# A two-layer mixture-of-experts network: six pairs' outputs added in DRAM, and the experts' weights read in 16 KB runs

## The chip, the cores and the metric

The kernel runs on one core of one Trainium2 chip. The metric is device time in microseconds for one whole execution. The median of three runs before is 1957.69 us (1956.69 to 1958.7).

## The reference, cut to what matters

Two streams pass through two layers: 512 latent tokens `x` ("l") and 256 context tokens ("c"), 1024 wide, all in fp32. A layer is a token mixer (short convolution, retention, windowed attention) and then a mixture of 16 experts, in which each expert picks its own tokens. The second layer has no context stream after the mixer. The part that the change touches:

```
def expert_choice_ffn(h, w_router, w_gate, w_up, w_down):
    n_tok, d_model = h.shape[1], h.shape[2]
    cap = CAPACITY_FACTOR * n_tok // N_EXPERTS          # 64 latent or 32 context tokens per expert
    aff = jax.nn.softmax((h @ w_router).astype(jnp.float32), axis=-1)
    gate, idx = lax.top_k(jnp.swapaxes(aff, 1, 2), cap)
    xs = jax.vmap(lambda hb, ib: hb[ib])(h, idx)
    a = jnp.einsum('becd,edf->becf', xs, w_gate)
    u = jnp.einsum('becd,edf->becf', xs, w_up)
    y = jnp.einsum('becf,efd->becd', jax.nn.silu(a) * u, w_down) * gate[..., None].astype(h.dtype)
    def scatter(ib, yb):
        return jnp.zeros((n_tok, d_model), yb.dtype).at[ib.reshape(-1)].add(yb.reshape(-1, d_model))
    return jax.vmap(scatter)(idx, y)
...
        h_l = modulate(rms_norm(x, norm2_g[l]), sh2, sc2)
        x = x + g2 * expert_choice_ffn(h_l, w_router[l], w_gate[l], w_up[l], w_down[l])
        if need_ctx:
            h_c = modulate(rms_norm(ctx, norm2_g[l]), csh2, csc2)
            ctx = ctx + cg2 * expert_choice_ffn(h_c, w_router[l], w_gate[l], w_up[l], w_down[l])
```

Each expert has three weight matrices of 1024 x 1024 fp32, 4 MiB each: 201 MB a layer.

## The kernel before, in words

**Experts.** `experts` works on eight pairs of experts. A pair's 128 rows (64 tokens for each of its two experts) are one tile; in layer 0, 128 context rows serve two pairs. For a pair it runs three products: `gate`, `up` and `down`, each over eight slices of 128 of the contracted dimension (`matrix`, with `lat_mm` and, for the context, `cx_mm`). The tokens are the weights that TensorE holds, the experts' weights stream past them. `times` multiplies the activated gate by `up`, `turned` transposes the product (eight transposes, four more for the context), and `down` takes it from there. `columns` transposes gathered rows and `modulate` scales them into `xT`. TensorE's order in this stage is written out by hand (`manual_schedule`):

```
            for p in range(7):
                rows(p + 2)          # gathers, on POOL
                gate(p + 1)
                turned(p)
                silu(p + 1)
                if p:
                    add(p - 1)
                inputs(p + 2)
                down(p)
                up(p + 1)
            add(6)
            turned(7)
            if two:                  # layer 0
                down(7)
                add(7)
```

**Outputs.** `down` scales its result by the token's gate and `g2` and splits it into a high and a low part (`yH`, `yL`, `ycH`, `ycL`). `add` builds a one-hot matrix of the pair's token numbers on VectorE and multiplies it with both parts on TensorE: 16 matmuls for the latent tokens (L1295, L1296), 8 for the context (L1305, L1306), each pair of them added into the residual `xe` in SBUF by VectorE (L1297, L1308). In layer 0, `xe` is loaded from the residual's DRAM copy `xres_d` (L1317) ahead of the first pair.

**Inputs.** In layer 0 the normalised rows lie in DRAM (`xn_d`), and `gather` fetches a pair's rows by an indirect DMA from POOL (L1047); its two buffers are shared by latent and context rows. In layer 1 the scaled rows (`scaled`) stay in SBUF as `xn`, and `gather_pe` picks them by a one-hot product on TensorE (L1092).

**Weights.** A `Ring` of tiles of 2 MiB ([128, 4, 1024]) holds the experts' weights, six tiles in layer 0. `ring_loads` gives the order: `gate`, `up` of a pair, then the next pair's `gate`, then `down`; four tiles to a matrix. SP issues a load (L1422) when its tile has been read. Row 128 j + p of a half matrix goes to partition p, slot j (`"(j p) n -> p j n"`), in runs of 4 KB. Some late tiles of layer 1 are loaded slot by slot (L1428).

**Selection and start.** `Norm2` transposes the residual and multiplies by the router's weights, `top` finds each expert's tokens, `slots_l` and `slots_c` turn the lists into columns (`idx_l`, `idx_c` for the gathers, `slot_l`, `sidx_c`, `gate_c` for the outputs). The modulation vectors come from `mod_half` and `mod_gen` (`w_mod` in tiles of 512 KB); `mod_cols` transposes them into the columns `A2`, `B2` by which `modulate` scales. At the very start SP loads the tokens (L282) and then small rows (`c`, `c_ctx`, `norm1_g`, `norm2_g`, `conv_w`, `final_g`, L1469 to L1474), which one transpose (L1476) turns into `cols`; everything behind needs it.

Except in the experts' loop, a scheduler orders each engine's instructions by the program's order and the tiles' dependencies, and two DMAs that write the same DRAM tile wait for each other.

Of the kernel before, what the change touches and what calls it, by code (L numbers as in the profile page):

```python
# [59 lines left out]
GLATE = 1  # L60
FINE = (9, 10, 11, 12)
# [26 lines left out]
def kernel(ctx_stack: ExitStack, tc: tile.TileContext, x, c, ctx, c_ctx, w_mod, b_mod, norm1_g,  # L88
# [58 lines left out]
    mod_d = [[dram.tile([2, 2048], F32, name=f"mod{l}{b}") for b in range(3)] for l in range(2)]  # L147
    A1, B1, A2, B2 = ([[cst.tile([128, KC], F32, name=f"{n}{l}{s}") for s in "lc"] for l in range(2)]
# [89 lines left out]
    def mod_cols(l, b, m, pp):  # L238
        ps = pp.tile([128, 4, 4, 32], F32, name="ps_mc", tag="t", bufs=4)
        for s in range(4):  # L240
            PE.transpose(ps[:, s].rearrange("p q r -> p (q r)"), m[:, 128 * s:128 * s + 128], ident)
        for r in range(2):
            v = ps[:, :, :, r].rearrange("p s q -> p q s")

            def o(t):
                return t[l][r].rearrange("p (q s) -> p q s", q=2)

            def g(t):
                return t[l].rearrange("p (q s) -> p q s", q=2)
            if b == 0:  # L250
                DVE.tensor_copy(o(B1), v[:, 0:2])
                DVE.scalar_tensor_tensor(o(A1), v[:, 2:4], 1.0, g(n1col), op0=OP.add, op1=OP.mult)
            elif b == 1:
                DVE.tensor_copy(o(B2), v[:, 2:4])
            else:
                DVE.scalar_tensor_tensor(o(A2), v[:, 0:2], 1.0, g(n2col), op0=OP.add, op1=OP.mult)
# [633 lines left out]
    class Norm2:  # L890
# [9 lines left out]
        def half(self, nh):  # L900
            s, p, pp, x, R = self.s, self.p, self.pp, self.x, self.R
            for t in range(NT[s]):
# [4 lines left out]
                for j in range(4):  # L907
                    PE.transpose(ps[:, j], xs[:, 128 * j:128 * j + 128], ident)
# [33 lines left out]
        def scaled(self, xn):  # L942
            for t in range(NT[self.s]):
                ACT.activation(xn[:, t], self.x[:, t], AF.Copy, scale=self.m[:, 1, t:t + 1])
# [46 lines left out]
    def slots_l(rp, p, pp, R, lst):  # L991
# [17 lines left out]
        for a, src in enumerate((R.tok_l, va)):  # L1009
            for half in range(2):  # L1010
                PE.matmul(ps[64 * half:64 * half + 64, 8 * a:8 * a + 8], src, ident[0:16, half:16:2],
                          start=True, stop=True)
        R.idx_l = rp.tile([128, 8], I32, name="idx_l")
# [4 lines left out]
    def slots_c(rp, pp, R, lst):  # L1018
        val, fi = lst
        ps = pp.tile([128, 512], F32, name="ps_r", tag="r", bufs=1)  # L1020
        for q in range(4):
# [4 lines left out]
                      tile_position=(0, 32 * q))  # L1026
        R.idx_c = rp.tile([128, 4], I32, name="idx_c")
# [32 lines left out]
    def columns(l, s, xs, ep, nb, bank):  # L1060

        xT = ep.tile([128, KC, 128], F32, name="xT" + s, bufs=nb)
        for g in range(2):
            ps = bank("ps_t").rearrange("p (j n) -> p j n", j=4)
            for j in range(4):
                PE.transpose(ps[:, j], xs[:, (4 * g + j) * 128:(4 * g + j + 1) * 128], ident)
# [91 lines left out]
    def experts(l, ep, ring, pp, R, xe, streams, late):  # L1158
# [66 lines left out]
        def turned(p):  # L1225

            aT[p] = E[0].tile([128, KC, 128], F32, name="aT", tag="aT", bufs=1)
            for h in range(2):
                ps = ptile("ps_t", "x").rearrange("p (j n) -> p j n", j=4)
                for j in range(4):  # L1230
                    PE.transpose(ps[:, j], sil[p][:, 512 * h + 128 * j:512 * h + 128 * j + 128], ident)  # L1231
# [4 lines left out]
            if two:  # L1236
                ps = ptile("ps_t", "bc").rearrange("p (j n) -> p j n", j=4)
                for j in range(4):
                    PE.transpose(ps[:, j], silc[p][:, 128 * j:128 * j + 128], ident)
# [24 lines left out]

        def down(p, fill=None):
            Dn = [ptile("ps_d", "a") for _ in range(2)]
            DC = ptile("ps_dc", "ac") if two else None
            for _ in matrix(Dn, DC, aT[p], lambda k, e: aTc[p][:, k % 4, 2 * e + k // 4, :], fill=fill):
                pass
            yH = E[0].tile([128, D], F32R, name="yH", bufs=1)  # L1270
# [39 lines left out]
        with tc.manual_schedule(engines={mybir.EngineType.PE}):  # L1310
            if two:
# [4 lines left out]
                for s in streams:  # L1316
                    POOL.dma_start(xe[s], xres_d[s].rearrange("(t p) d -> p t d", p=128))  # L1317
# [20 lines left out]
            for p in range(7):  # L1338
# [4 lines left out]
                if p:  # L1343
# [30 lines left out]
    def ring_loads(l):  # L1374
# [3 lines left out]
        for wsrc, p in order:  # L1378
            for kh in range(2):
                for e in range(2):  # L1380
                    yield wsrc[l, 2 * p + e, 512 * kh:512 * kh + 512, :].rearrange("(j p) n -> p j n", p=128)
# [59 lines left out]
    for l in range(2):  # L1441
# [3 lines left out]
        if True:  # L1445
# [3 lines left out]
            POOL.dma_start(R.wr, w_router[l].rearrange("(j p) n -> p j n", p=128))  # L1449
# [13 lines left out]
            with ExitStack() as s2:  # L1463
                pp = s2.enter_context(tc.tile_pool(name=f"pp{l}", bufs=1, space=PSUM))
                m0 = router_cols(l, streams, pp, R) if l else None
                if l == 0:
# [5 lines left out]
                    SP.dma_start(rows[32:48], norm2_g.rearrange("l (r p) -> (l r) p", p=128))  # L1472
# [128 lines left out]
            with ExitStack() as s2:  # L1601
# [32 lines left out]
                def passes():  # L1634
# [23 lines left out]
                    def select_l():  # L1658
# [4 lines left out]
                        slots_l(rp, p, pp, R, lst)  # L1663
# [6 lines left out]
                    if two:  # L1670
# [16 lines left out]
                        def select_c():  # L1687
# [4 lines left out]
                            slots_c(rp, pp, R, (yield from top(p, pp, R, "c", 32)))  # L1692
# [109 lines left out]
```

## Time and profile before

| | us |
|---|---|
| median of 3 runs | 1957.69 |
| the profiled execution | 1955.63 |
| its span | 1953.8 |
| TensorE busy | 1815.8 (93%) |
| VectorE busy | 722.0 (37%) |
| ScalarE busy | 489.6 (25%) |
| GpSimd busy | 286.5 (15%) |

Times are in microseconds from the span's start unless ns is said. PE is TensorE's matmuls, PEld its weight loads, DVE VectorE, ACT ScalarE, POOL GpSimd, and SPq, POOLq the queues from which SP and GpSimd issue. A name such as `ps_d<-ring,aT` is output, then the streamed and the held operand. L1297 is line 1297 of the kernel. Matmuls overlap, so the sum of their durations is more than the time that they take; the starts of groups are the better measure.

### The profile page before, as it was taken

What the parts mean: (1) busy time and instruction counts of PE and PEld (TensorE: products, weight loads), DVE (VectorE), ACT (ScalarE), POOL (GpSimd) and SP (SyncE); (2) the same over time, 40 slices, a digit from 0 to 9 for tenths busy, and PEclk for the clock granted to TensorE, in tenths of its full rate; (3) what the DMA queues carried; (4) which work ended last, traced back from release to release, by engine and by line L of the source; (5) the groups of instructions that cost most, each with busy time, mean ns of one, the idle gap of its engine ahead of it and who ended that gap; (6) DMA issues with size and microseconds to landing.
All of it is one profiled execution on the core that took longest, in us unless ns stands there. A gap on an engine that the chain in (4) does not pass through costs nothing. (4 is left out here: it accounts for less than half of the span.)

```text
span 1953.8 us, 30558 instructions
## 1 busy us (share of the span) xinstructions
PE 1815.8 (93%) x12747; PEld 1040.3 (53%) x12747; DVE 722.0 (37%) x1785; ACT 489.6 (25%) x983; POOL 286.5 (15%) x309
## 2 busy tenths in 40 slices
PE   5899999999889999999999789999969999989986
PEld 2778777766423333333333488877744444433532
DVE  5645345663511213222223555446341122221214
ACT  3444343344201001001100345454321000000001
POOL 3323132343200000000000132323410000000000
PEclk9999999999889999999999999999979999999998
DMA  8453454267689999998897411211747999999994
GB/s 267 162 196 130 140 177 150 87 243 280 241 341 409 390 397 358 354 394 342 347 400 282 152 45 33 63 36 33 290 182 286 415 416 417 417 416 415 417 417 173
DMA packets 157761, 522.94 MB, mean 268 GB/s; under 512 B 8836, under 2 KB 31432, under 8 KB 157624
## 3 DMA queue, kind: packets, MB, share of 16 engines
q1 hardware_dynamic: 154200, 511.24, 68.4%
q0 software_dynamic: 3424, 9.75, 1.4%
q8 instruction: 100, 1.64, 0.3%
q14 instruction: 37, 0.30, 0.0%
HBM read 510.41 MB, written 10.55 MB: 267 GB/s over the span
## 5 line engine op out<-in xcount | busy, mean ns | idle before, releaser
L1102 PE MATMUL ps_g<-ring,xTl 128*32 128x512 f32 (+1 forms) x1472 | 244.3, 596 | 11.8 <-DMA ring<-in_w_gate_dram 10.5
L1102 PE MATMUL ps_u<-ring,xTl 128*32 128x512 f32 (+1 forms) x1536 | 236.7, 598 | 14.3 <-DMA ring<-in_w_up_dram 13.6
L1102 PE MATMUL ps_d<-ring,aT 128*32 128x512 f32 (+1 forms) x1536 | 234.7, 593 | 0.5 <-DMA ring<-in_w_down_dram 0.3
L1102 PEld LDWEIGHTS ps_g<-ring,xTl 128*32 128x32 f32 (+1 forms) x1472 | 75.7, 121 | 159.5 <-issue 133.1
L1102 PEld LDWEIGHTS ps_u<-ring,xTl 128*32 128x32 f32 (+1 forms) x1536 | 70.2, 120 | 168.0 <-issue 144.1
L351 PE MATMUL acc<-wH,hHl 128*128 128x256 f32 x512 | 151.6, 296 | 2.6 <-ACT wH L272 1.3
L352 PE MATMUL acc<-wH,hLl 128*128 128x256 f32 x512 | 144.7, 283 | 3.7 <-DVE hLl L341 3.7
L353 PE MATMUL acc<-wL,hHl 128*128 128x256 f32 x512 | 145.3, 284 | 1.2 <-DVE wL L273 1.1
L1102 PEld LDWEIGHTS ps_d<-ring,aT 128*32 128x32 f32 (+1 forms) x1536 | 68.6, 119 | 144.8 <-issue 142.4
L1235 ACT ACTIVATE aT<-ps_t 128x512 f32<-128x512 f32 x16 | 9.6, 598 | 495.3 <-PE ps_t L1231 495.3
L351 PEld LDWEIGHTS acc<-wH,hHl 128*128 128x128 f32 x512 | 97.4, 190 | 30.1 <-issue 23.7
L1274 DVE SCALAR_TENSOR_TENSOR ps_d<-ps_d,slot_l,g 128x512 f32<-128x512 f32 x32 | 24.3, 759 | 227.8 <-PE ps_d L1102 226.1
L1214 DVE TENSOR_TENSOR sil<-ps_u,sil 128x512 f32<-128x512 f32 x32 | 22.1, 692 | 232.6 <-PE ps_u L1102 232.6
L1233 DVE COPY aT<-ps_t 128x512 f32<-128x512 f32 x16 | 11.1, 691 | 261.8 <-PE ps_t L1231 261.8
L352 PEld LDWEIGHTS acc<-wH,hLl 128*128 128x128 f32 x512 | 97.5, 191 | 4.6 <-DVE hLl L341 4.6
L353 PEld LDWEIGHTS acc<-wL,hHl 128*128 128x128 f32 x512 | 97.5, 191 | 4.0 <-DVE wL L273 2.3
L273 POOL TENSOR_TENSOR wL<-wraw,wH 128x512 fp32r<-128x512 f32 x44 | 57.6, 1308 | 273.1 <-ACT wH L272 263.3
L675 DVE TENSOR_REDUCE mc<-ps_s 128x1 f32<-128x513 f32 (+2 forms) x80 | 55.2, 690 | 84.5 <-PE ps_s L672 52.7
L1275 ACT ACTIVATE yH<-ps_d 128x512 fp32r<-128x512 f32 x32 | 19.1, 597 | 263.9 <-DVE ps_d L1274 263.9
L677 ACT ACTIVATE P<-ps_s,mc 128x513 f32<-128x513 f32 (+2 forms) x80 | 55.1, 689 | 97.0 <-DVE mc L675 96.9
L1153 POOL TENSOR_TENSOR x<-z,xTl 128x512 f32<-128x512 f32 x3 | 4.2, 1413 | 512.4 <-ACT z L1152 512.4
L272 ACT ACTIVATE wH<-wraw 128x512 fp32r<-128x512 f32 x88 | 55.1, 629 | 90.2 <-PE acc L352 37.4
(482 smaller groups left out, 3393.7 us busy)
## 6 DMA issues: line engine op xcount, KB each, us to landing
ring<-in_w_up_dram SPq DMA_DIRECT2D x64, 2048.0 KB, 13.7
ring<-in_w_gate_dram SPq DMA_DIRECT2D x61, 2048.0 KB, 13.8
ring<-in_w_down_dram SPq DMA_DIRECT2D x61, 2048.0 KB, 16.0
wm<-in_w_mod_dram SPq DMA_DIRECT2D x96, 512.0 KB, 4.6
wraw<-in_w_in_dram SPq DMA_DIRECT2D x44, 512.0 KB, 3.7
wraw_o<-in_w_out_dram SPq DMA_DIRECT2D x24, 512.0 KB, 4.5
ring<-in_w_gate_dram SPq DMA_DIRECT2D x12, 512.0 KB, 5.6
ring<-in_w_down_dram SPq DMA_DIRECT2D x12, 512.0 KB, 14.7
```

What stands on the lines that cost most here:

```text
L272: ACT.activation(H, src, AF.Copy)
L273: sub_eng().tensor_sub(L, src, f32(H))
L351: PE.matmul(ps, aH, bH, start=start, stop=False)
L352: PE.matmul(ps, aL, bH, start=False, stop=False)
L353: PE.matmul(ps, aH, bL, start=False, stop=stop)
L675: DVE.tensor_reduce(mc[:, 0:1], sc, AX.X, OP.max, negate=True)
L677: ACT.activation(P[:, :nk + 1], sc, AF.Exp, bias=mc[:, 0:1], accum_out=mc[:, 1:2])
L1102: PE.matmul(G[h][c:c + n], lhs[:, k, c:c + n], W[e][:, j, 512 * h:512 * h + 512], start=(k == 0), stop=(k == KC - 1), tile_position=(0, c))
L1214: DVE.tensor_mul(sil[p][:, hs], U[h], sil[p][:, hs])
L1233: DVE.tensor_copy(aT[p][:, 4 * h:4 * h + 4], ps)
L1274: DVE.scalar_tensor_tensor(Dn[h], Dn[h], R.slot_l[:, 1, p:p + 1], R.g2[:, hs], op0=OP.mult, op1=OP.mult)
L1275: ACT.activation(yH[:, hs], Dn[h], AF.Copy)
```

## The change

The experts' outputs of pairs 0 to 5 in layer 0 are no longer added by TensorE: `down` ends in `scatter`, in which VectorE writes the scaled output as fp32 into SBUF and POOL issues four indirect DMAs (two experts, latent and context) that add the rows to the residual in DRAM. `xe` is loaded after pair 5's; pairs 6 and 7 are added as before. `slots_l` and `slots_c` make the index columns for it.

The experts' weights are laid out so that partition p holds rows 4 p to 4 p + 3 of a half matrix. What is contracted with them takes the same order: the transposes read every fourth element, the second norm's vector is loaded in that order, the router's weights too, and layer 1's `scaled` writes its rows in it.

```diff
+NACC = 6
...
     def mod_cols(l, b, m, pp):
-            PE.transpose(ps[:, s].rearrange("p q r -> p (q r)"), m[:, 128 * s:128 * s + 128], ident)
+            PE.transpose(ps[:, s].rearrange("p q r -> p (q r)"), m[:, s::4] if b else m[:, 128 * s:128 * s + 128], ident)
...
     class Norm2: half
-                    PE.transpose(ps[:, j], xs[:, 128 * j:128 * j + 128], ident)
+                    PE.transpose(ps[:, j], xs[:, j::4], ident)
         def scaled(self, xn):
             for t in range(NT[self.s]):
-                ACT.activation(xn[:, t], self.x[:, t], AF.Copy, scale=self.m[:, 1, t:t + 1])
+                o, i = xn[:, t], self.x[:, t]
+                if xn is not self.x:
+                    o, i = o.rearrange("q (g j p) -> q g j p", g=2, j=4), i.rearrange("q (g p j) -> q g j p", g=2, j=4)
+                ACT.activation(o, i, AF.Copy, scale=self.m[:, 1, t:t + 1])
...
     slots_l
+        if two:
+            PE.matmul(ps[0:64, 16:24], R.tok_l, ident[0:16, 1:16:2], start=True, stop=True)
+            R.to_l = two.tile([64, 2, 8], I32, name="to_l")
+            for e in range(2):
+                DVE.tensor_copy(R.to_l[:, e], ps[0:64, 16 * e:16 * e + 8])
         R.idx_l = rp.tile([128, 8], I32, name="idx_l")
...
     slots_c
+        R.to_c = ra.tile([64, 2, 8], I32, name="to_c")
+        for h in range(2):
+            hs = slice(32 * h, 32 * h + 32)
+            for e in range(2):
+                PE.matmul(ps[hs, 20 + 8 * e:28 + 8 * e], fi, ident[0:16, e:16:2], start=True, stop=True,
+                          tile_position=(0, 32 * h))
+        for e in range(2):
+            DVE.tensor_scalar(R.to_c[:, e], ps[0:64, 20 + 8 * e:28 + 8 * e], 2.0, hm[0:64, 0, 1:2], op0=OP.mult,
+                              op1=OP.subtract)
...
     columns
-                PE.transpose(ps[:, j], xs[:, (4 * g + j) * 128:(4 * g + j + 1) * 128], ident)
+                PE.transpose(ps[:, j], xs[:, 512 * g + j:512 * g + 512:4], ident)
     turned
-                    PE.transpose(ps[:, j], sil[p][:, 512 * h + 128 * j:512 * h + 128 * j + 128], ident)
+                    PE.transpose(ps[:, j], sil[p][:, 512 * h + j:512 * h + 512:4], ident)
-                    PE.transpose(ps[:, j], silc[p][:, 128 * j:128 * j + 128], ident)
+                    PE.transpose(ps[:, j], silc[p][:, j::4], ident)
...
+        def scatter(p, Dn, DC):
+            y = ep.tile([128, D], F32, name="y", tag=("yH", "yL")[p % 2], bufs=1)
+            yc = ep.tile([128, 512], F32, name="yc", tag=("ycH", "ycL")[p % 2], bufs=1)
+            for h in range(2):
+                hs = slice(512 * h, 512 * h + 512)
+                DVE.scalar_tensor_tensor(y[:, hs], Dn[h], R.slot_l[:, 1, p:p + 1], R.g2[:, hs], op0=OP.mult, op1=OP.mult)
+            DVE.scalar_tensor_tensor(yc, DC, R.gate_c[:, p:p + 1], R.g2c, op0=OP.mult, op1=OP.mult)
+            for e in range(2):
+                es = slice(64 * e, 64 * e + 64)
+                for dst, idx, src in ((xres_d["l"][:, :], R.to_l, y),
+                                      (xres_d["c"].rearrange("t (h n) -> (t h) n", h=2), R.to_c, yc)):
+                    POOL.indirect_dma_start(out=dst, out_offset=bass.IndirectOffsetOnAxis(ap=idx[:, e, p:p + 1], axis=0),
+                                            in_=src[es, :], in_offset=None, compute_op=OP.add)
+            if p == NACC - 1:
+                for s in streams:
+                    POOL.dma_start(xe[s], xres_d[s].rearrange("(t p) d -> p t d", p=128))
         down
+            if two and p < NACC:
+                scatter(p, Dn, DC)
+                return
...
     experts, ahead of pair 0 in layer 0
-                for s in streams:
-                    POOL.dma_start(xe[s], xres_d[s].rearrange("(t p) d -> p t d", p=128))
     experts, the loop
-                if p:
+                if p > (NACC if two else 0):
                     add(p - 1)
     ring_loads
-                    yield wsrc[l, 2 * p + e, 512 * kh:512 * kh + 512, :].rearrange("(j p) n -> p j n", p=128)
+                    yield wsrc[l, 2 * p + e, 512 * kh:512 * kh + 512, :].rearrange("(p j) n -> p j n", j=4)
...
-            POOL.dma_start(R.wr, w_router[l].rearrange("(j p) n -> p j n", p=128))
+            for kh in range(2):
+                POOL.dma_start(R.wr[:, 4 * kh:4 * kh + 4], w_router[l, 512 * kh:512 * kh + 512].rearrange("(p j) n -> p j n", j=4))
...
-                    SP.dma_start(rows[32:48], norm2_g.rearrange("l (r p) -> (l r) p", p=128))
+                    for i in range(4):
+                        SP.dma_start(rows[32 + 4 * i:36 + 4 * i], norm2_g[i // 2, 512 * (i % 2):512 * (i % 2) + 512]
+                                     .rearrange("(p j) -> j p", j=4))
```

## Rows read from the trace of the kernel before

**Rows 1.** The page's 40 slices: TensorE and the DMA engines, busy tenths.

```profile
PE   5899999999889999999999789999969999989986
...
DMA  8453454267689999998897411211747999999994
```

**Rows 2.** Windows: busy PE, PEld, DVE, ACT, POOL; PEclk, DMA share, GB/s.

```profile
1500.00:1900.00 400.00, 377.01 (x1884) 171.56 (x1880) 81.22 (x151) 30.39 (x59) 0.00 (x0) 0.98 1.02 416
575.00:1060.00 485.00, 484.78 (x4304) 173.75 (x4306) 108.55 (x197) 46.80 (x95) 7.51 (x8) 1.00 0.96 374
```

**Rows 3.** Timeline of TensorE in layer 0: start, length, instruction.

```profile
599.84 1.92 PE L1102 MATMUL ps_d<-ring,aT 128*32 128x512 f32 x16
...
620.47 1.90 PE L1102 MATMUL ps_u<-ring,xTl 128*32 128x512 f32 x16
...
663.18 0.50 PE L1295 MATMUL ps_s<-yH,OH 128*128 128x512 f32 x1
...
668.88 1.25 PE L1066 MATMUL ps_t<-ident,xsl 128*128 128x128 f32 x8
670.07 1.92 PE L1102 MATMUL ps_d<-ring,aT 128*32 128x512 f32 x16
...
741.34 1.92 PE L1102 MATMUL ps_d<-ring,aT 128*32 128x512 f32 x16
```

**Rows 4.** Timeline of TensorE in layer 1, first transposes of two pairs.

```profile
1624.94 1.09 PE L1231 MATMUL ps_t<-ident,sil 128*128 128x128 f32 x8
...
1685.37 1.09 PE L1231 MATMUL ps_t<-ident,sil 128*128 128x128 f32 x8
```

**Rows 5.** Waits in layer 1, 1490 to 1920: total, times, longest.

```profile
PEld ps_g L1102 <- DMA ring<-in_w_gate_dram: 16.0, 7, 3.5
...
PEld ps_u L1102 <- DMA ring<-in_w_up_dram: 7.6, 2, 4.0
```

**Rows 6.** Timeline around `turned` and its copies, layer 0.

```profile
598.39 0.66 PE L1066 MATMUL ps_t<-ident,xsl 128*128 128x128 f32 x4 [0.22 <-ACT aTc L1241]
...
1015.01 1.09 PE L1231 MATMUL ps_t<-ident,sil 128*128 128x128 f32 x8
...
1016.73 0.60 ACT L1241 ACTIVATE aTc<-ps_t 128x512 f32<-128x512 f32 x1
```

**Rows 7.** Line L1047, the gathers: duration min/median/max, and landing.

```profile
L1047 POOL DMA_INDIRECT xsl<-xn_l,idx_l x8: 935/942/1037, 503.5 to 882.0; - x8
...
DMA to landing us min/median/max: 4.2/7.9/8.8
```

**Rows 8.** Tile `ps_t`: weight loads of `turned`, ns min/median/max.

```profile
L1231 PEld LDWEIGHTS ps_t<-ident,sil x128: 138/140/144, 596.2 to 1912.7; 128*128 128x128 f32 x128
```

**Rows 9.** Tile `qsum` and line L935: VectorE's reductions of 64 elements.

```profile
L120 DVE TENSOR_REDUCE qsum<-ident x1: 240/240/240, 2.9 to 2.9; 128x16 f32<-128x64 f32 x1
...
L935 DVE TENSOR_REDUCE rm<-aff_l x2: 219/220/220, 482.5 to 1435.8; 128x4 f32<-128x64 f32 x2
```

**Rows 10.** DMA queues, 1500 to 1900: packets, MB, share of 16 engines.

```profile
DMA packets 41799, 166.22 MB, mean 416 GB/s; under 512 B 1267, under 2 KB 1267, under 8 KB 41780
...
q1 hardware_dynamic: 41780, 165.95, 102.2%
```

**Rows 11.** DMA queues from 1180 to 1230.

```profile
DMA packets 2115, 2.15 MB, mean 43 GB/s; under 512 B 64, under 2 KB 2112, under 8 KB 2112
...
q1 hardware_dynamic: 2112, 2.10, 13.3%
```

**Rows 12.** The page's packets over the whole span.

```profile
DMA packets 157761, 522.94 MB, mean 268 GB/s; under 512 B 8836, under 2 KB 31432, under 8 KB 157624
```

**Rows 13.** Waits of SP at the start, and the first transpose.

```profile
SPq L1474 <- DMA xt<-in_x_dram: 1.9, 1, 1.9
...
14.24 0.34 PE L1476 MATMUL ps_t<-ident,rows 68*128 68x68 f32 x1 [14.24 <-DMA rows<-in_final_g_dram]
```

**Rows 14.** Line L1014, the copy that makes `idx_l`.

```profile
L1014 DVE CAST idx_l<-ps_r x2: 153/160/167, 503.0 to 1452.2; 128x8 int32<-128x8 f32 x2
```

More of the change, by code (lines that the diff above doesn't have):

```diff
@@ L989, in top, with slots_l @@
         return val, fi
-    def slots_l(rp, p, pp, R, lst):
+    def slots_l(rp, p, pp, R, lst, two):
         val, fi = lst
@@ L1016, in slots_l, with slots_c @@
         DVE.tensor_copy(R.slot_l, ps[:, :16].rearrange("p (a e) -> p a e", a=2))
-    def slots_c(rp, pp, R, lst):
+    def slots_c(rp, pp, R, lst, ra):
         val, fi = lst
@@ L1662, in select_l @@
                         lst = yield from top(p, pp, R, "l", 64)
-                        slots_l(rp, p, pp, R, lst)
+                        slots_l(rp, p, pp, R, lst, two and ra[0])
                         if two:
@@ L1691, in select_c @@
                             yield from keep("c", nc2, xc)
-                            slots_c(rp, pp, R, (yield from top(p, pp, R, "c", 32)))
+                            slots_c(rp, pp, R, (yield from top(p, pp, R, "c", 32)), ra[0])
                         aft = select_c()
```

## The prediction

> **What bounds the kernel now.** I read the page's slices first [rows 1]: TensorE is busy nearly everywhere, while the DMA engines are full only in two stretches, slices 13 to 21 and 32 to 39. These are the expert stages of layer 0 and layer 1, so I then read the windows by stage [rows 2]. In layer 0's window TensorE is busy 484.78 of 485 us at 374 GB/s: TensorE bounds it. In layer 1's window the rate is 416 GB/s and the DMA share is over 1, while TensorE is idle for 23 of 400 us: the transfers bound it. Next came the timeline of TensorE. In layer 0 one pair takes 70.2 us where two gathered inputs are turned less, and 71.3 us where the context's rows are turned too (from 599.84, the start of a `down`, to 670.07 and 741.34 [rows 3]); the mean is 70.75. In layer 1 a pair takes 60.4 us (1624.94 to 1685.37 [rows 4]), and the waits view lists 23.6 us before weight loads that a ring transfer ended [rows 5]. The chain of waits agrees in kind: in layer 1 it runs back through ring transfers, in the last stage of selection through VectorE, so that whatever layer 0 gains or the start loses reaches the end in full, as layer 1's work begins with layer 0's residual.
>
> **Part 1: adds 0 to 5 leave TensorE.** `add` runs eight times in layer 0 and six go. One stands between the first L1295 and the next transpose: 663.18 to 668.88, 5.70 us [rows 3]. Nothing else runs on TensorE in that time, and TensorE is the bound, so 6 x 5.70 = 34.2 us go. VectorE's 12 adds, ACT's copies and the one-hot rows go too and are worth nothing, as both engines are idle most of that window (VectorE is busy 108.55 of 485 us [rows 2]).
>
> What is late next: the add also covered the copies of `turned` before `down`. ACT ends the copy of `aTc` 2.3 us after the first transpose (1016.73 plus 0.60, against 1015.01 [rows 6]); the 20 transposes of `turned` and `inputs` take 20 x 1.09 / 8 = 2.7 us [rows 6], so the cover is just there. At p = 0, which has no add, the wait was 0.22 us [rows 6]. I take 0.4 us a pair for bank waits, 2.4 us in all (0 to 6 x 1 us).
>
> Is TensorE still the bound? A pair without its add takes 65.05 us. Its weights are 12 loads of 2 MiB, 25.17 MB, 60.5 us at 416 GB/s. The scatter adds 768 KB a pair, 1.9 us at that rate, twice that if the destination is read as well: 64.3 us. That is still below 65.05, by little, and Part 3 widens it. The ring's six tiles hold the difference within a pair. The residual's load (3 MB, 7.6 us of transfer) moves from before the first gathers to after scatter 5; it is needed four matrices of 20.6 us later, so it costs nothing.
>
> The new wait: the two adding DMAs into the same DRAM tile follow each other, so POOL holds the second until the first has landed. Behind it on POOL stand the other adding DMAs and then the gather of pair p+3. That gather must land before `inputs(p+3)`, which is `up`, `gate` and `turned` after `down(p)`: 20.6 + 20.6 + 1.6 = 42.8 us (a matrix is 599.84 to 620.47 [rows 3]). An indirect DMA issues in 0.94 us and lands in 7.9 us [rows 7]. Two links and the gather make 3 x 8.9 = 26.7 us, so 16 us are spare, and the wait costs nothing. The trace has no adding DMA; at 4.2 us [rows 7] it is shorter, and from about twice 7.9 us it shows (a rival).
>
> **Part 2: strided transposes.** Each transpose loads its data as weights, and these are now read at every fourth element. The loads take 140 ns [rows 8], and 8 transposes take 1.09 us [rows 6], 136 ns each, so the load sets the pace. On the path: 96 in `turned` and 96 in `columns` of layer 0, 80 in `Norm2`, 16 in `mod_cols`, 288 in all; the 64 of layer 1's `turned` lie beside waits for transfers. No row shows a strided weight load. The nearest is VectorE's reduction at steps of 32 elements: 240 ns, against 220 ns for as many elements in order [rows 9]. That is 0.3 ns an element, or 40 ns for 128. I take half, 20 ns: 5.8 us (0 to 11.5 by that row, 40 us if a load doubles, the far end that I keep; a gain is excluded, as nothing gets shorter).
>
> The Trainium skill, page "SBUF — State Buffer", section "Door 1: The DMA port swizzle", says that memory lines have 16 bytes and that an access which goes to a new line each time pays; a step of four fp32 values does that. It speaks against this change, gives no price, and the VectorE row bears it out only weakly. It is the first rival.
>
> In layer 1 `scaled` reads its input at a step of four in four ACT instructions of 1024 elements; I take nothing (0 to 4 x 1024 x 0.3 ns = 1.2 us by VectorE's row).
>
> **Part 3: 16 KB runs.** Each partition's four rows of a ring tile are now one run in DRAM and in SBUF. In layer 1's window, 40513 packets of 4 KB took 102.2% of 16 queues for 400 us [rows 10], or 161 ns each; in the window where packets are 1 KB, 2048 took 13.3% of 50 us, or 52 ns [rows 11]. The line through both is 15.2 ns a packet plus 35.6 ns per 1000 bytes: 599 ns for 16 KB, against 645 ns for four of 4 KB, 7% less. Whether a 16 KB run stays one packet no row shows; pieces that touch are joined up to 4 KB at least: the 126192 packets of 2 to 8 KB hold 3.94 KB on average [rows 12] (522.94 MB, less 23 MB in the smaller ones and 2 MB of instructions), so some 9400 are of 2 KB, and the 80 `w_mod` tiles of `mod_gen`, two touching pieces of 2 KB in each partition, would alone make 20480. If the run stays whole, the 415 us in which layer 1's transfers are full shrink by 29 us, but TensorE allows less: a pair's 60.4 us hold one wait of 2 to 3.5 us, so it needs 57 to 58 by itself, and all ring waits together are 23.6 us [rows 5]. I take 17 us, three quarters of that, since a stream at the pace of its consumer still makes some waits (0 if packets stay 4 KB; 23.6 the other end). In layer 0 TensorE is the bound, and it gives nothing.
>
> **Part 4: the start.** `norm2_g` came in one DMA of 16 rows and comes in four, whose source steps by four elements. Each element becomes a packet of its own: 4 x 512. These stand in the queue ahead of `conv_w`, `final_g` and the first `w_mod`, and TensorE's first transpose waits for the last of the rows, at 14.24 us [rows 13]. If the four rows of a destination take four queues, each gets 512 packets; at the line's 15.2 ns that is 7.8 us; over all 16 queues 1.9 us; at the price of a 1 KB packet 26.5 us. SP also issues three more DMAs, and it is held by earlier landings (L1474 waited for `xt` [rows 13]), so `final_g` can't slip ahead. I take 6 us, nearer to the four-queue end; all stages behind follow, so it is paid in full.
>
> **Part 5: selection.** `slots_l` gains a matmul and two VectorE copies of 0.16 us [rows 14] ahead of `idx_l`, for which the gather waits: 0.4 us. In `slots_c` the same stands beside TensorE's first `up`. The router's two DMAs are hidden.
>
> **Sum.** -34.2 + 2.4 + 5.8 - 17 + 6 + 0.4 = -36.6 us. The profiled execution took 1955.6 us, around its span of 1953.8; the median of the three is 1957.7, 2.1 more. 1955.6 - 36.6 + 2.1 = **1921 us**.
>
> **Rivals.**
>
> A. A strided weight load doubles (140 ns more each): 40 instead of 5.8 us, 1955 us, the gain of the adds eaten. For: the load paces the transposes. Against: VectorE's row. It decides from 147 ns more a load ((36.6 + 5.8) / 288): from there nothing is left.
>
> B. POOL's queue takes over, the slower side. An adding DMA reads, adds and writes; if it lands after 3 x 7.9 us, two links and the gather take 2 x 24.6 + 8.9 = 58 us against 42.8, and five pairs' inputs come 15.2 us late: +76, 1997 us. It shows from twice the gather's landing and makes the kernel slower from about 2.4 times. For: the queue is strictly in order. Against: only 64 rows each, and 16 us of slack.
>
> C. The runs are cut into 4 KB packets, or the larger ones run no faster: 1921 + 17 = 1938 us. For: every packet of the ring is one 4 KB row now. Against: the pieces of `w_mod` are joined [rows 12].
>
> D. Small packets cost as much as 1 KB ones: 20 us more at the start, 1941 us. The Trainium skill, page "DMA: Bandwidth & Descriptors", section "Rules for kernel authors", says that a last dimension which isn't contiguous becomes one descriptor per element; the count used above follows from the source's step alone, and no row here shows such a packet.
>
> **Chances.** Forecast 0.50 (its own range 1903 to 1938), A 0.13, B 0.06, C 0.15, D 0.12, other mishaps that end slower 0.04. A measurement of this kernel tells 0.2% (4 us) from no change. Faster: forecast, C, D and a third of A, 0.81. Same: most of the rest of A, 0.08. Slower: B, the others and A's far end, 0.11. The range 1900 to 1957 leaves out those slower cases and a sum in which every cost is at its low end, 0.05.
>
> **What would show it.** Layer 0's pair at 65 to 66 us with TensorE still near 100%, and no L1295 before `add(6)`. A weight load of the transposes at 140 to 180 ns; 280 would be A. POOL's wait before the gathers for TensorE, not for an adding DMA; else B. Packets in layer 1 a quarter in number at over 430 GB/s and a pair in about 57 us; else C. The first transpose at about 20 us; at 40, D. A pair of layer 0 over 70 us, or DMA waits in its `gate`, would make the forecast wrong at its largest term.

## The result and the profile after

The changed kernel took 1928.38 us (median of 4, 1925.89 to 1929.08) beside 1957.19 for the kernel before: a ratio of 0.9851, 95% interval 0.9839 to 0.9863. In a second set it took 1925.05 beside 1956.43, 0.9837 (0.9822 to 0.9852). The median of all eight is 1926.2, against which the variants below are set. The forecast was 1921.

The profiled execution has a span of 1924.1 us, 29.7 less than before. Its page: TensorE's slices, the DMA engines', and the packets.

```profile
PE   4899999999889999999999889999969999999986
...
DMA  7554264257659999999997411110747999999993
...
DMA packets 90351, 527.63 MB, mean 274 GB/s; under 512 B 11300, under 2 KB 33880, under 8 KB 66408
```

Slices 13 to 21 are now full in both rows, where before the DMA row stood at 8 and 9 [rows 1]. Packets fall from 157761 to 90351 [rows 12]. The same by windows, layer 0's and layer 1's experts (busy PE, PEld, DVE, ACT, POOL; clock, DMA share, GB/s):

```profile
575.00:1037.00 462.00, 456.85 (x4192) 150.61 (x4188) 50.86 (x90) 35.68 (x78) 43.56 (x34) 1.00 1.01 409
1480.00:1880.00 400.00, 385.02 (x1928) 179.50 (x1924) 85.60 (x159) 30.39 (x59) 0.00 (x0) 0.99 1.01 428
```

Layer 0's transfers have become as full as TensorE (share 1.01, where it was 0.96), and layer 1's run at 428 GB/s, where it was 416 [rows 2]. TensorE's timeline in layer 0, the starts of `down` for pairs 0, 1, 2, 6 and 7, and two waits between the last two:

```profile
604.83 1.06 PE L1124 MATMUL ps_d<-ring,aT 128*32 128x512 f32 x8
...
669.47 1.07 PE L1124 MATMUL ps_d<-ring,aT 128*32 128x512 f32 x8
...
735.99 1.49 PE L1124 MATMUL ps_d<-ring,aT 128*32 128x512 f32 x12
...
996.10 0.64 PE L1124 MATMUL ps_d<-ring,aT 128*32 128x512 f32 x4 [0.27 <-ACT sil L1228]
...
1009.68 0.64 PE L1124 MATMUL ps_d<-ring,aT 128*32 128x512 f32 x4 [2.11 <-DMA ring<-in_w_down_dram]
...
1020.93 0.64 PE L1124 MATMUL ps_u<-ring,xTl 128*32 128x512 f32 x4 [0.74 <-DMA ring<-in_w_up_dram]
...
1050.01 0.64 PE L1124 MATMUL ps_d<-ring,aT 128*32 128x512 f32 x4
```

A pair takes 64.64 or 66.52 us; from pair 0's `down` to pair 6's it is 391.27, or 65.2 a pair, where it was 422.19, or 70.4. The step from pair 6 to pair 7 went the other way, from 50.36 to 53.91: there a `down` and an `up` wait for weights. In layer 1 (the `turned` of two pairs, as in [rows 4]) a pair of 60.43 us takes 56.55. Pairs differ there, and the next one takes 60.01; the mean of five is 60.2 before (1566.64 to 1867.67) and 58.2 after (1546.23 to 1837.18). The two `turned`:

```profile
1603.70 1.23 PE L1253 MATMUL ps_t<-ident,sil 128*128 128x128 f32 x8
...
1660.25 1.23 PE L1253 MATMUL ps_t<-ident,sil 128*128 128x128 f32 x8
```

Put in order of time, before and after, the whole difference of the profiled spans is found:

| stretch | before | after | difference |
|---|---|---|---|
| start to pair 0's `down` | 599.84 | 604.83 | +5.0 |
| pair 0's to pair 6's `down` | 422.19 | 391.27 | -30.9 |
| pair 6's to pair 7's `down` | 50.36 | 53.91 | +3.5 |
| to layer 1's first `ps_x` (1454.25, 1434.15) | 381.86 | 384.14 | +2.3 |
| to the end | 499.55 | 489.95 | -9.6 |
| sum | 1953.8 | 1924.1 | -29.7 |

### The profile page after: what moved, and what is told of

Its sections match the earlier page's. It is cut to its first block, busy times and chain, and to the rows that moved or that the text cites. A ratio compares the mean times of both kernels' runs of the same rounds, so it can differ in the third digit from the quotient of the medians.

```text
span 1924.1 us, 30120 instructions
## 1 busy us (share of the span) xinstructions
PE 1783.6 (93%) x12613; PEld 1023.5 (53%) x12613; DVE 664.1 (35%) x1681; ACT 481.9 (25%) x965; POOL 321.1 (17%) x335
## 2 busy tenths in 40 slices
DMA packets 90351, 527.63 MB, mean 274 GB/s; under 512 B 11300, under 2 KB 33880, under 8 KB 66408
## 5 line engine op out<-in xcount | busy, mean ns | idle before, releaser
L1124 PE MATMUL ps_u<-ring,xTl 128*32 128x512 f32 (+1 forms) x1536 | 243.3, 601 | 14.2 <-DMA ring<-in_w_up_dram 13.5
L1124 PE MATMUL ps_g<-ring,xTl 128*32 128x512 f32 (+1 forms) x1472 | 239.0, 594 | 4.0 <-DMA ring<-in_w_gate_dram 2.8
L1114 PE MATMUL ps_x<-OT,xn 128*128 128x128 f32 x512 | 67.1, 297 | 8.1 <-DVE OT L1106 8.1
L1131 PE MATMUL ps_uc<-ring,xTc 128*32 128x512 f32 x512 | 72.9, 592 | 0.0
```

What stands on the lines that cost most here:

```text
L1114: PE.matmul(ps[:, j], R.xn[:, t, c0:c0 + 128], OT[:, t], start=(t == 0), stop=(t == 3))
L1124: PE.matmul(G[h][c:c + n], lhs[:, k, c:c + n], W[e][:, j, 512 * h:512 * h + 512], start=(k == 0), stop=(k == KC - 1), tile_position=(0, c))
L1131: PE.matmul(gcx[32 * b:32 * b + 32], lhs_c(k, e), W[e][:, j, 512 * h:512 * h + 512], start=(k == 0), stop=(k == KC - 1), tile_position=(0, ...
```

## The experiments

The table says where the time is, not which part of the change brought it. The theory that I took into the experiments was that the parts add up, as in the forecast; the rival was that the 16 KB runs are what lets layer 0 have the gain of the additions.

**The additions alone.** The changed kernel with the old order everywhere:

```diff
-   yield wsrc[...].rearrange("(p j) n -> p j n", j=4)
+   yield wsrc[...].rearrange("(j p) n -> p j n", p=128)
-   PE.transpose(ps[:, j], sil[p][:, 512 * h + j:512 * h + 512:4], ident)
+   PE.transpose(ps[:, j], sil[p][:, 512 * h + 128 * j:512 * h + 128 * j + 128], ident)
...
```

> The DRAM additions of six pairs (with the reload of the residual after the sixth) without any other part of the change: weights in runs of 4 KB, all steps of 1, the start as before. Theory 1 (the parts add up: TensorE sets the pace of a pair of layer 0, so what it no longer does comes off the time): the six pairs give 31 to 34 us, the reload's collision takes 3.5 back, so 1926 to 1930 us, as fast as the whole change; a pair of layer 0 takes 63 to 65 us between two starts of down. Theory 2 (without the additions the ring of weights sets the pace of layer 0, and the 16 KB runs are what lets it follow): 1935 to 1945 us, with PE waiting for the ring 2 to 3 us a pair in layer 0.

Measured: 1948.71 us, 0.9964 of before (0.9954 to 0.9974), a gain of 8 us and not of 30. Both numbers of theory 1 failed; the time is even beyond theory 2's. TensorE's waits from 605 to 1070 us in this kernel (total, times, longest):

```profile
PE ps_g L1121 <- DMA ring<-in_w_gate_dram: 12.6, 7, 5.7
```

The kernel before has no wait for the ring in this stretch. The starts of `down` for pairs 0, 5, 6 and 7:

```profile
604.70 1.06 PE L1121 MATMUL ps_d<-ring,aT 128*32 128x512 f32 x8
...
941.70 0.64 PE L1121 MATMUL ps_d<-ring,aT 128*32 128x512 f32 x4
...
1016.90 0.64 PE L1121 MATMUL ps_d<-ring,aT 128*32 128x512 f32 x4 [0.36 <-ACT sil L1225]
...
1066.48 1.06 PE L1121 MATMUL ps_d<-ring,aT 128*32 128x512 f32 x8
```

Five pairs take 67.4 us each (337.0 in all), where the whole change has 65.5, and the pair with the reload takes 75.2. The DMA queues from 605 to 945 us (packets, MB, share of 16 engines), first of the kernel before, then of this one:

```profile
q1 hardware_dynamic: 31364, 124.58, 93.5%
q0 software_dynamic: 927, 3.34, 2.5%
```

```profile
q1 hardware_dynamic: 32074, 127.41, 93.7%
q0 software_dynamic: 2608, 7.60, 8.7%
```

The software queue, which carries gathers and additions, takes 8.7% of the engines, where it took 2.5%. Over 340 us and five pairs, 6.2% is 4.2 us of all sixteen engines a pair. The ring is left with 127.41 MB in 340 us, 375 GB/s, and 25.17 MB at that rate are 67.2 us: the pair. The window of this kernel (last three columns: clock, DMA share, GB/s) shows what a full stretch looks like:

```profile
605.00:945.00 340.00, 332.60 (x3028) 106.56 (x3024) 37.61 (x69) 24.77 (x58) 34.49 (x27) 1.00 1.03 398
```

So 5.7 us of TensorE were exchanged for 4.2 us of the DMA engines, and the ring became the bound. The row of before already had it: a share of 0.96 [rows 2] of a 70.4 us pair is 67.6 us of packets, 65.6 by the 1.03 of this full stretch, so that a pair of 65 us was full before anything was added to it. (This profiled execution came to pair 0's `down` 4.9 us late and took 3.5 us more than its kernel's median; only times within layer 0 are read from it.)

**The runs alone.** The changed kernel with `NACC = 0` and the residual's load ahead of pair 0, as before.

> The new order of the weights with all that goes with it (16 KB runs, steps of 4 in the transposes, the scaled rows, the router's weights, the four loads of norm2_g) with no pair added in DRAM and the residual loaded ahead of pair 0 as before. Theory 1 (sum of the differences between the two traces: start +5.0, head of layer 1 +2.3, experts of layer 1 -9.6, strided transposes of layer 0 between +1 and +5): 1956 to 1960 us, no gain by itself. Theory 2 (16 KB runs also speed up layer 0, where the ring waits once the transfers are faster): 1948 to 1954 us. By the prediction's terms (-17 +5.8 +6 +0.4) it would be 1952.

Measured: 1953.61 us, 0.9979 (0.9970 to 0.9989), 3.4 us less than before, between the two theories. In its trace layer 0 gains nothing (473.9 us from pair 0's `down` to pair 7's, before 472.55), layer 1's experts take 489.6 us, and pair 0's `down` is 3.9 late. Alone the parts give 8.3 and 3.4 us, together about 30: some 18 us exist only where both are present.

**What an adding DMA costs.** The kernel of the additions alone, with plain writes in their place:

```diff
-   in_=src[es, :], in_offset=None, compute_op=OP.add)
+   in_=src[es, :], in_offset=None)
```

> The additions alone as in e1_adds_only (runs of 4 KB), but the indirect DMAs write their rows instead of adding them: it leaves out the sum with what stands in DRAM. In e1_adds_only the DMA engines were busy throughout the six pairs and the software queue took 8.7% of them. Theory 1 (DMA work sets the pace there, and an accumulating row costs a read and a write where a written one costs a write): the queue's share falls to about 5%, a pair by 1.5 to 2.5 us, the whole to 1936 to 1941 us against 1948.7. Theory 2 (accumulating costs the engines no more than writing): 1948 to 1950 us, and the share stays.

Measured: 1939.07 us (1936.56 to 1940.76), as theory 1 has it. Its queues in the same window, and pairs 0 and 5:

```profile
q1 hardware_dynamic: 33041, 131.26, 96.6%
q0 software_dynamic: 2195, 7.22, 5.3%
```

```profile
599.65 1.06 PE L1121 MATMUL ps_d<-ring,aT 128*32 128x512 f32 x8
...
927.92 1.49 PE L1121 MATMUL ps_d<-ring,aT 128*32 128x512 f32 x12
```

The queue's share falls to 5.3%, and five pairs take 328.3 us, 65.7 each. The packets are still of 4 KB and the engines still full (share 1.02), but the ring gets 131.26 MB instead of 127.41 and nearly follows TensorE, which needs 65.2 us a pair without strides (326.2 for the same five, in the run on the step of 4 below). 8.7% of 67.4 us less 5.3% of 65.7 is 2.4 us a pair for the adding alone. The pairs follow the load on the DMA engines, with TensorE's work unchanged.

**TensorE's own pace.** The whole change with half of the ring's bytes:

```diff
-   SP.dma_start(t, src)
+   SP.dma_start(t[:, 0:2], src[:, 0:2])
-   W[e][:, j, 512 * h:512 * h + 512]
+   W[e][:, j % 2, 512 * h:512 * h + 512]
```

> The whole change with half of every expert weight tile left out of the loads (each partition gets 8 KB of its 16, and the matrix multiplications use those twice): every instruction of TensorE stays, the ring's bytes are halved, and so what remains of the expert stages is TensorE's own pace. Theory 1 (with 16 KB runs TensorE sets the pace of a pair of layer 0 and all but about 8 us of layer 1): pairs of layer 0 stay at 64 to 66 us, the waits of the prologue of layer 0 (7.7) and of layer 1 (7.8) go, 1905 to 1915 us. Theory 2 (DMA sets the pace of layer 0 after the change too): pairs of 58 to 62 us, under 1895 us.

Measured: 1903.22 us (1900.34 to 1906.71), somewhat under theory 1's range, and its reading of layer 0 holds to the hundredth. Pairs 0, 6 and 7, and the window of layer 0:

```profile
600.53 1.06 PE L1124 MATMUL ps_d<-ring,aT 128*32 128x512 f32 x8
...
991.79 1.62 PE L1124 MATMUL ps_d<-ring,aT 128*32 128x512 f32 x12 [0.27 <-ACT sil L1228]
...
1041.60 0.64 PE L1124 MATMUL ps_d<-ring,aT 128*32 128x512 f32 x4
```

```profile
605.00:945.00 340.00, 338.25 (x3120) 111.58 (x3112) 35.73 (x63) 23.45 (x53) 33.44 (x25) 1.00 0.61 213
```

With a DMA share of 0.61 the six pairs take 391.26 us, as with the whole change at 1.01. So with 16 KB runs TensorE sets the pace there. In layer 1 the mean of the same five pairs is 57.2 us. Layer 1's experts end 478.3 us after their first `ps_x`, where it was 499.55 before and 489.95 after: 21.2 us of layer 1 hung on transfers, and the runs gave back 9.6.

**The reload's place.** The whole change with the residual loaded ahead of pair 0:

```diff
-   if p == NACC - 1:
-       for s in streams:
-           POOL.dma_start(xe[s], xres_d[s]...)
```

> The whole change with the residual loaded ahead of pair 0, as before the change, and not after the sixth pair; what the six pairs added in DRAM is thereby left out of the result. It is the price of the reload at its place. Theory 1 (the reload takes the ring's share of the DMA engines while down(6) and up(7) wait for weights): 2.5 to 4.5 us less than the whole change, 1924 to 1926 us, and from down(6) to down(7) 50.5 us instead of 53.9. Theory 2 (the longer last pair has another reason): 1928 us and 53.9.

Measured: 1921.55 us (1919.24 to 1925.14), 4.7 under 1926.2. Pair 6 to pair 7 takes 49.80 us:

```profile
993.02 1.06 PE L1124 MATMUL ps_d<-ring,aT 128*32 128x512 f32 x8 [0.27 <-ACT sil L1228]
...
1042.82 0.64 PE L1124 MATMUL ps_d<-ring,aT 128*32 128x512 f32 x4
```

So the reload costs 4.1 us of those 53.91, or 3.0 of the 52.85 in the second profile of the changed kernel. The median alone doesn't tell this price, since pair 0's `down` also comes 3.1 us earlier in this profile, at 601.75. With half of the ring's bytes and the reload at its place the stretch takes 49.81 us too, so the cost lies in the engines that the two share. The landing in the changed kernel:

```profile
L1303 POOL DMA_DIRECT2D xel<-xres_l x1: 857/857/857, 975.7 to 975.7; - x1
...
DMA to landing us min/median/max: 29.4/29.4/29.4
```

The latent tokens' 2 MB of the 3 took 29.4 us to land, beside a ring that already filled the engines, where 13.5 us are enough behind the ring's last load (with seven pairs, below). In the meantime `down(6)` and `up(7)` wait for weights.

**The price of the step of 4.**

```diff
-   PE.transpose(ps[:, j], xs[:, 512 * g + j:512 * g + 512:4], ident)
+   PE.transpose(ps[:, j], xs[:, (4 * g + j) * 128:(4 * g + j + 1) * 128], ident)
...
```

> The whole change, but the transposes of the expert stage (inputs of layer 0, products of both layers) read 128 neighbouring columns instead of every fourth one, so rows and weights no longer belong together and the output is another: it is the price of the step of 4 alone. Weight loads of transposes go back from 209 to 140 ns. Theory 1 (the loads lie beside matmuls, 6 to 18 ns of each transpose reach the end): 288 transposes, 2 to 5 us less, 1923 to 1926 us. Theory 2 (the full 69 ns of each load reach the end, as in rival A): 20 us less, 1908. Theory 3 (nothing reaches it): 1928.

Measured: 1922.75 us (1922.35 to 1923.26), 3.5 under 1926.2: theory 1. The weight loads of `turned`, in the changed kernel and in this one (ns, min/median/max):

```profile
L1253 PEld LDWEIGHTS ps_t<-ident,sil x128: 195/209/220, 600.8 to 1881.0; 128*128 128x128 f32 x128
```

```profile
L1253 PEld LDWEIGHTS ps_t<-ident,sil x128: 137/140/144, 601.4 to 1877.5; 128*128 128x128 f32 x128
```

A load takes 69 ns more with the step, yet six pairs take 390.0 us instead of 391.27: 1.27 us for 128 transposes, 10 ns each. The runs alone agree (423.47 for these pairs, before 422.19). The four transposes of `silc` and the next one on TensorE, first before the change, then after it, show how a longer load can cost so little:

```profile
597.10 0.60 PE L1239 MATMUL ps_t<-ident,silc 128*128 128x128 f32 x4
597.53 0.64 PE L1066 MATMUL ps_t<-ident,xsl 128*128 128x128 f32 x4
```

```profile
601.87 0.64 PE L1261 MATMUL ps_t<-ident,silc 128*128 128x128 f32 x4
602.35 0.64 PE L1088 MATMUL ps_t<-ident,xsl 128*128 128x128 f32 x4
```

In a row, transposes start 0.11 us apart before and 0.12 after, less than one load's 140 and 209 ns: the loads overlap each other. The rest of the 3.5 us lies mostly in the stretch of the reload (51.74 instead of 53.91), which differs by 1 us between two profiles of the same kernel (53.91, 52.85), and the changed kernel's two medians are 3.3 apart, so that rest isn't shown; layer 1's experts take 490.0 us with and without.

**The start.** One contiguous load of `norm2_g`, turned by four small transposes:

```diff
-   for i in range(4):
-       SP.dma_start(rows[32 + 4 * i:36 + 4 * i], norm2_g[...].rearrange("(p j) -> j p", j=4))
+   SP.dma_start(r2, norm2_g.rearrange("l (h n) -> (l h) n", h=2))
...
+   for j in range(4):
+       PE.transpose(ps[:, 64 + 4 * j:68 + 4 * j], r2[:, j::4], ident[:4, :4])
```

> The whole change with the four 4-byte-wise loads of norm2_g replaced by one contiguous load of 4 rows of 512 and four small transposes with a step of 4; the first transpose then waits for rows that come as early as before. If the late start is carried through to the end one to one (theory 1), it gives back 4.5 to 5.5 us: 1923 to 1924 us against 1928.4. If it is taken up on the way by the load of weights, which starts at a time of its own (theory 2), 1927 to 1928.5 us.

Measured: 1922.89 us (1918.42 to 1924.31), 3.3 under 1926.2 and 5.5 under the first set. The first transpose comes at 14.50 instead of 19.81 (first fence: the changed kernel; second: this one), and pair 0's `down` at 599.99 instead of 604.83:

```profile
19.81 0.35 PE L1520 MATMUL ps_t<-ident,rows 68*128 68x68 f32 x1 [19.81 <-DMA rows<-in_final_g_dram]
```

```profile
14.50 0.32 PE L1519 MATMUL ps_t<-ident,rows 52*128 52x52 f32 x1 [14.50 <-DMA rows<-in_final_g_dram]
```

In these two profiles the start is carried through to the first pair in full; to the end the medians don't tell 3.3 from 5. Over all profiles the first transpose comes at 14.1 to 14.8 us without the four loads and at 18.7 to 20.5 with them. Pair 0's `down` spreads more, 599.7 to 604.7 without and 601.8 to 605.9 with them (600.5 with half the bytes), so the 5.0 of the table holds to a few us only.

**Packets of 8 KB.**

```diff
-   SP.dma_start(t, src)
+   for a in (0, 2):
+       SP.dma_start(t[:, a:a + 2], src[:, a:a + 2])
```

> The whole change, but each weight tile is loaded in two halves, so that a packet brings 8 KB of a partition and not 16; the order of the weights and all strided reads stay. A 4 KB packet took 159 ns and a 16 KB one 611 ns, a line of 8 ns and 36.8 ns per 1000 bytes, by which 8 KB take 310 ns, 1.4% more per byte than in 16 KB. Theory 1 (the gain of the runs is this fixed time per packet): a pair of layer 0 hardly changes (the DMA engines have under 1% to spare there), layer 1 loses about 1% of its transfer-bound part, 2 to 5 us more than the whole change. Theory 2 (8 KB are as good as 16): within 1 us of it. Theory 3 (it is the order in memory, a whole row block per partition, that counts, and halves lose it): 8 us or more, near e1_adds_only with 1948.

Measured: 1927.54 us (1924.31 to 1931.13), 1.3 over 1926.2 and 2.5 over the set beside it: theory 3 is out, the other two can't be told apart by the time. The queue in layer 1 can: packets, MB and share of 16 engines over 400 us, first of the changed kernel from 1480, then of this one.

```profile
q1 hardware_dynamic: 12057, 171.06, 100.4%
```

```profile
q1 hardware_dynamic: 23300, 169.06, 100.9%
```

By share x 16 x 400 us / MB, one MB takes an engine 39.41 us in 4 KB packets [rows 10], 38.20 in 8 KB and 37.56 in 16 KB. A fixed 10.1 ns a packet with 36.94 us per MB, fixed by the first and the last, gives 38.17 for the middle one.

**Seven pairs, and both mends.** `NACC = 7`, with `add(6)` for layer 1 only:

```diff
-NACC = 6
+NACC = 7
-   add(6)
+   if not two:
+       add(6)
```

> The whole change with seven pairs instead of six added in DRAM: add(6) falls away too, and the residual is reloaded after the seventh pair, when the ring has few or no loads of layer 0 left to be held up. Theory 1 (TensorE's 5.7 us of add(6) come off, and so do the about 3 us that the reload took from the ring in pair 7): 1919 to 1921 us against 1928.4. Theory 2 (the reload now lands late, add(7) waits for it, and the gain is given back there): 1926 to 1935 us, with a wait on the reload at the head of add(7).

Measured: 1916.79 us (1915.85 to 1920.53), 9.4 under 1926.2: theory 1, even a little better. The reload is now issued 10 us after the ring's last load for layer 0, its 2 MB for the latent tokens land in 13.5 us, and the first addition that needs it comes 23 us after its issue, later than they land. From pair 0's `down` to layer 1's first `ps_x` this kernel takes 818.1 us and the changed one 829.3, so the gain lies there and not in the start's spread:

```profile
1039.29 0.86 POOL L1303 DMA_DIRECT2D xel<-xres_l  x1 [3.28 <-DMA xres_l<-y,to_l]
...
1062.82 0.68 DVE L1340 TENSOR_TENSOR xel<-xel,ps_s 128x512 f32<-128x512 f32 x1
```

Together with the start's mend:

> The whole change with the two mends together: the contiguous load of norm2_g (e3_start: 5.5 us less than the whole change) and seven pairs added in DRAM (e4_seven: 11.6 less). They lie in different stages, so theory 1 (the two add up): 1911 to 1913 us. Theory 2 (part of what the seventh pair gave was the start's spread from run to run, which here can't come twice): 1914 to 1917 us.

Measured: 1912.67 us (median of 5, 1909.92 to 1913.38), 0.9773 of before (0.9759 to 0.9786). Theory 1 holds within 1 us (1926.2 - 9.4 - 3.3 is 1913.5), and the stretch above takes 818.1 us again. This version beats both kernels, by 44 us and by 13.5. The changed kernel once more, beside it:

> The whole change once more, unaltered, beside the other two on the same chip, so that they can be set against it: 1926 to 1930 us is expected, with the start of the first down anywhere from 601 to 606 us.

Measured: 1925.05 us (1924.68 to 1926.53), 1 us under the lower end; pair 0's `down` at 604.26.

## Why the prediction was right, and where not

The direction was right, and the time was 7 us too low (-36.6 against -29.7 in the profiled execution). The largest term came out nearly as forecast, but its mechanism, that TensorE bounds layer 0 once the adds are gone, holds only with the 16 KB runs, for which the prediction booked nothing in layer 0. Two errors cancel there, which is luck. By its own steps:

**Part 1, the six adds: the size right, the reason incomplete.** -34.2 + 2.4 stood against -30.9 for pair 0 to 6, which also holds the strided transposes of these pairs (without them 390.0 us, or -32.2); bank waits were named at 0.4 us a pair, and the trace has 1.8 us of `aTc` waits in the six and 0.7 of `aT` waits behind them. But the question "Is TensorE still the bound?" was answered with 64.3 us of transfers against 65.05, for 4 KB packets, and the additions alone take 67.4. The count was short: the gathers' share (2.5% of the engines) was left out, and the ring was priced at layer 1's undisturbed 416 GB/s. The text said that Part 3 widens the margin; in truth it makes it.

**The reload at nothing: wrong.** It was argued from its 7.6 us and the four matrices, 82 us, until it is needed (in the trace the first addition into it comes 67 us after its issue). That was the wrong question: not whether it is late, but whom it delays. It cost 3.0 to 4.1 us. In the additions alone its pair takes 7.8 more than the mean of the five ahead of it (75.2 against 67.4), which is the whole of its 3 MB at some 400 GB/s; no run takes it away there.

**POOL's wait at nothing: right, rival B false.** A link of two adding DMAs (line 1299: issue, then landing) and the chain of pair 0 on POOL:

```profile
L1299 POOL DMA_INDIRECT xres_l<-y,to_l x12: 1409/1414/1519, 625.9 to 965.5; - x12
...
DMA to landing us min/median/max: 9.2/10.1/12.3
```

```profile
625.88 1.52 POOL L1299 DMA_INDIRECT xres_l<-y,to_l  x1 [19.47 <-DVE y L1293]
...
635.65 1.42 POOL L1299 DMA_INDIRECT xres_l<-y,to_l  x1 [6.52 <-DMA xres_l<-y,to_l]
...
669.81 1.01 POOL L1069 DMA_INDIRECT xsc<-xn_c,idx_c  x1 [29.15 <-PE ps_t L1088]
```

They land in 10.1 us, where a gather took 7.9 [rows 7], but after the last one POOL still waits 29.15 us for TensorE to free a buffer before it gathers. (By the rival's own sum, its wait would have eaten the whole gain from 2.5 times the gather's landing, not 2.4.)

**Part 2, the stride: half the size in the pairs, and the reading wrong.** I took 5.8 us, from 20 ns each, "so the load sets the pace". It doesn't: 1.09 us for eight includes the tail of the last one, and in a row they start 0.11 us apart. The load got 69 ns longer, half of rival A's 140, and 10 ns of it reached the end, for the transposes of the pairs; that of `Norm2` wasn't tried by itself. That a load estimated at less than a third of its growth gave a term of the right order is luck; rival A is false. The Trainium skill, page "SBUF — State Buffer", section "Door 1: The DMA port swizzle", says that an access that goes to a new 16-byte line each time pays. The trace agrees (140 to 209 ns), but nearly all of it overlaps TensorE's other work. On ACT it shows in full: `scaled` with a step of 4 (the first row, `xn`) against in order:

```profile
L950 ACT ACTIVATE xn<-x,rm 128x1024 f32<-128x1024 f32 x4 | 8.2, 2102 | 1.3 <-DVE rm L183 1.3
...
L950 ACT ACTIVATE x<-x,rm 128x1024 f32<-128x1024 f32 x4 | 4.5, 1140 | 1.6 <-DVE rm L183 1.6
```

That is 0.96 us an instruction, 3.8 for the four, where I took nothing and had 1.2 as the upper end. One of the four lies on the path to layer 1's selection: the chain runs through the first, at 1414.19, which ACT does ahead of `aff_l`; the other three come behind it. The runs alone, with the same step, lose 0.9 us in that stretch, so it explains them; of the whole change's 2.3 the rest stays open.

**Part 3, 16 KB runs: the term that missed most.** -17 was forecast for layer 1 and -9.6 came. The cap was read from weight loads' waits, 23.6 us [rows 5], where TensorE itself, measured with half the bytes, could gain 21.2; the engines' time per byte fell by 4.7% and not 7, as a packet's fixed part is 10.1 ns and not 15.2, and the rate rose by 2.9%, 416 to 428 GB/s, which is 12 us of the 415. The ring's waits that are left:

```profile
PEld ps_u L1124 <- DMA ring<-in_w_up_dram: 6.8, 2, 3.5
PEld ps_g L1124 <- DMA ring<-in_w_gate_dram: 6.7, 5, 3.4
```

"In layer 0 it gives nothing" was wrong as a statement about the part: from pair 0's `down` to pair 7's the additions alone take 461.8 us and the whole change 445.2, so it gives 16.6. The sum did not suffer, since Part 1 had already booked that gain as its own. Rival C is false: packets of layer 1 fell from 41780 to 12057.

By the Trainium skill, page "Perfetto Trace Analysis", section "Roofline", one core alone is held by its 16 DMA engines at about 435 GB/s. The 428 of layer 1's window agrees: longer runs have little more to give here.

**Part 4, the start: 6 forecast, 5.0 measured, by another path.** The first transpose comes at 19.81, as the forecast of 6 us has it, but not because the engines have small packets to carry: from 12 to 18 us their share is 0.22. What takes the time is SP's issuing. Its timeline, and the four loads by themselves (ns, min/median/max):

```profile
5.59 9.91 SPq L1515 DMA_DIRECT2D rows<-in_norm_g_dram  x4
...
17.75 1.93 SPq L220 DMA_DIRECT2D wm<-in_w_mod_dram  x4
```

```profile
L1515 SPq DMA_DIRECT2D rows<-in_norm_g_dram x4: 341/1670/3940, 5.6 to 14.4; - x4
```

The 9.91 us from the first of the four loads to the last hold 7.6 us of issuing (0.34, 3.94, 2.21 and 1.13) and a wait of 2.2 for the tokens' landing, for which SP waited before too. One contiguous load took 0.32 before and takes 0.25 in the mended start. `w_mod`, issued behind them, starts at 17.75 where it was 10.75, and the first transpose waits for the rows behind them (19.81, above). Why SP issues so slowly stays open: the first of the four went in 0.34 us, and the contiguous `conv_w` behind them took 1.82, where it took 0.30 before, which speaks against a fixed price per element. Rival D is false.

**Part 5:** 0.4 us is within the 2.3 above and can't be told from it.

## What to carry to other kernels

When work goes off the engine that bounds a stage, price it on the one that takes it over and compare the sum with the room that is left there, with all that the stage already sends. Two edits that are small alone may each remove what hides the other; test them apart and together before one of them is dropped. A transfer put into a full stage delays what the stage itself loads, whenever its result is due: here 3 MB cost 3 to 8 us.

## What the runs showed of the hardware

An adding indirect DMA of 64 rows took POOL 1.41 us to issue, a writing one 0.89 and a gather of 128 rows 0.94 [rows 7]; the adding cost the DMA engines 2.4 us a pair over the write. Four loads of 512 elements each, taken at a step of four in DRAM, held SP for 0.34 to 3.94 us each, 7.6 in all, with the DMA engines mostly idle. A step of four fp32 elements lengthened a TensorE weight load by half, 140 to 209 ns, but the spacing of transposes by 10 ns only; it lengthened an ACT instruction from 1.14 to 2.10 us. A packet of the ring cost a DMA engine 10.1 ns beside 36.94 us per MB.
